# Second layer's first FFN: 19 pairs of up chunks as 2x2 block products with seven multiplications, its modulation computed in other FFNs

## The chip, the core and the metric

The program runs on one core of one Trainium2 chip. The metric is the device time of one execution in microseconds (us). Engines: TensorE (PE, with its weight loads PEld), VectorE (DVE), ScalarE (ACT), GpSimd (POOL) and SyncE (SP), which issues the DMAs here.

## The reference, cut to what matters

Two transformer blocks are computed on 256 tokens ("latent") with 256 context tokens beside them in the first block, model width 1024. The first block has two layers; each layer has a feed-forward network (FFN), a token mixer and a second FFN. Everything is float32.

```python
def _swiglu(h, w1, w3, w2):                       # w1, w3: 1024 x 2816, w2: 2816 x 1024
    return (jax.nn.silu(h @ w1) * (h @ w3)) @ w2
def _modulation(cond, w, b):                      # nine vectors of 1024 per layer
    m = jax.nn.silu(cond) @ w + b
    return [m[:, None, j * D_MODEL:(j + 1) * D_MODEL] for j in range(N_MOD)]
...
    for l in range(DEPTH):                        # DEPTH = 2
        ml = _modulation(c, w_ada[l], b_ada[l]); mc = _modulation(c_ctx[None], w_ada[l], b_ada[l])
        ffn1 = (ffn1_w1[l], ffn1_w3[l], ffn1_w2[l])
        lat = lat + 0.5 * ml[2] * _swiglu(_modulate(lat, norm_ffn1_g[l], ml[0], ml[1]), *ffn1)
        cx = cx + 0.5 * mc[2] * _swiglu(_modulate(cx, norm_ffn1_g[l], mc[0], mc[1]), *ffn1)
        ...                                       # token mixer, then ffn2 in the same way
```

## The kernel before

Activations lie transposed, features on partitions and tokens along the free axis: columns 0 to 255 are the latent tokens, 256 to 511 the context. A float32 product is made of three TensorE passes over operands split into a rounded part (hi) and a remainder (lo): hi times hi, hi times lo, lo times hi (`mm3`, lines 294 to 296).

**Weights** come in 544 chunks of up to 128 x 1024 in the order of `plan()`. For each, SP loads a raw tile (four buffers), ACT writes hi (line 145, six buffers) and DVE writes lo = raw - hi (line 156, five buffers). `take` hands the next chunk to the matmuls; `ahead_hi` and `ahead_lo` convert ahead as far as the buffers go.

**An FFN** has 22 pairs of up chunks: pair j holds 128 columns of w1 and the same of w3. They go in thirds of 8, 7 and 7 pairs (`THIRDS`), and each third is followed by eight w2 chunks that take the third's results. An up chunk is 8 k-blocks x 3 passes = 24 matmuls of 512 columns. `gated` (lines 519 to 527) then makes g = silu(first) * second: silu on ACT, the product on DVE (line 523), hi on ACT (line 525), lo on DVE (line 526). The results of w2 chunks are added to xT by DVE (line 417). In a layer's first FFN the first two pairs are computed together with the norm ahead of it (`norm_group`, `tail`).

**The order** is written out by hand: the schedule is manual, and each engine takes its instructions in the order in which the code issues them. `step` issues a chunk's matmuls, then the epilogue of the step before (`flush`), then conversions of hi (`ahead_hi`), one item of background work (`tick`), then conversions of lo (`ahead_lo`). There are six PSUM buffers `mm` of 512 columns, five temporaries `t`, and nine buffers `g`.

**Modulation.** The nine vectors of each layer come from 72 units of 128 outputs. A unit is one DMA of 512 KB and two DVE instructions over 1024 columns (line 279) with a read of the accumulator behind each. `ada` is a generator that does one unit per tick. The first layer's first FFN does the first layer's units 16 to 71, its second FFN does the second layer's units 0 to 39, and the second layer's first FFN does units 40 to 71.

Of the kernel before, what the change touches and what calls it, by code (L numbers as in the profile page):

```python
# [7 lines left out]
F32 = mybir.dt.float32  # L8
# [93 lines left out]


EARLY = 5
PACE = ([0, 1.25], [0, 1])


class Pair:


    def __init__(self, hi, lo=None):
        self.t = [hi, lo]
# [5 lines left out]
class Weights:  # L118


    def __init__(self, nc, flat, rawp, hlp, sizes, nraw, nhl):
        self.nc, self.flat, self.rawp, self.hlp = nc, flat, rawp, hlp
        self.sizes, self.nraw, self.nhl = sizes, nraw, nhl
        self.offs = np.concatenate([[0], np.cumsum(np.array(sizes) * 128)]).tolist()
        self.n = len(sizes)
        self.n_dma = self.n_hi = self.n_lo = self.n_take = 0
        self.raw, self.hl = {}, {}

    def dma_to(self, i):
        while self.n_dma <= min(i, self.n - 1):  # L130
# [6 lines left out]
            self.n_dma += 1  # L137

    def hi_to(self, i):
        while self.n_hi <= min(i, self.n - 1):  # L140
            j = self.n_hi
            self.dma_to(j)
            c = self.sizes[j]
            t = self.hlp.tile([128, 1024], F32R, tag="hi", name="hi", bufs=self.nhl)
            self.nc.scalar.activation(out=t[:, :c], in_=self.raw[j][:, :c], func=AF.Copy)  # L145
            self.hl[j] = Pair(t)
            self.n_hi += 1

    def lo_to(self, i):
        while self.n_lo <= min(i, self.n - 1):  # L150
            j = self.n_lo
            self.hi_to(j)
            c = self.sizes[j]
            t = self.hlp.tile([128, 1024], F32R, tag="lo", name="lo", bufs=self.nhl - 1)
            w = self.hl[j]
            self.nc.vector.tensor_tensor(  # L156
                out=t[:, :c], in0=self.raw.pop(j)[:, :c], in1=w[:, 0, :c].bitcast(F32), op=ALU.subtract)
            w.t[1] = t
            self.n_lo += 1
        self.dma_to(self.n_lo - 1 + self.nraw)  # L160

    def take(self, n):
        self.base = self.n_take
        self.lo_to(self.n_take + n - 1)
        r = [self.hl.pop(self.n_take + i) for i in range(n)]
        self.n_take += n
        return r

# [2 lines left out]
        self.ahead_lo(rate)  # L171

    def ahead_hi(self, rate=3):
        self.hi_to(min(self.n_hi + rate - 1, self.base + self.nhl - 1))

    def ahead_lo(self, rate=3):
        self.lo_to(min(self.n_lo + rate - 1, self.base + self.nhl - 2))


def build(tc, T):  # L180
    nc = tc.nc
    vo, nvec = vec_plan()
    sizes = [p[3] * p[5] for p in plan()]
    PS = bass.MemoryType.PSUM
    with ExitStack() as ctx, tc.manual_schedule():
        pool = lambda name, bufs, **k: ctx.enter_context(tc.tile_pool(name=name, bufs=bufs, **k))
# [7 lines left out]
        b1 = ctx.enter_context(ExitStack())  # L194
        hp = b1.enter_context(tc.tile_pool(name="hp", bufs=1))

        W = Weights(nc, T["wflat"], rawp, hlp, sizes, 4, 6)
# [33 lines left out]
        def drain(g):  # L231
            if g in side:
                for _ in g:
                    pass
                side.remove(g)
# [18 lines left out]
                    nc.vector.tensor_scalar(sl, sl, 0.5, None, ALU.mult)  # L254
            modn[l] = n1

        def ada(l, t0, t1, adap, lead):

            todo, tiles = list(range(t0, t1)), []

            def load():
                if todo:
                    t = adap.tile([128, 1024], F32, tag="ada", name="ada")
                    nc.sync.dma_start(out=t, in_=T["adaT"][l, todo.pop(0)])
# [8 lines left out]
            for j in range(t0, t1):  # L273
                if j > t0:
# [32 lines left out]
        def flush():  # L307
            while epis:
                epis.pop(0)()
# [202 lines left out]
            return ps  # L512


        def ffn(l, i, halves, ps4, gp, end, xepi=None):
            t1 = halves[-1][1]
            g = {}

            def gated(j, pa, pb):
# [11 lines left out]
            for ti, (j0, nj) in enumerate(THIRDS):  # L531
                for j in range(j0, j0 + nj):
                    if j < 2:
                        continue
# [7 lines left out]
                flush()  # L542
                X = [g.pop(j) for j in range(j0, j0 + nj)]
                lastt = ti == 2
                if lastt:
                    prime(AF.Sqrt)
                if lastt and xepi:
                    new_h2()
                for o in range(6 if lastt and end else 8):
                    (w,) = W.take(1)  # L550
                    p = mm_ps()
# [8 lines left out]
                    step(lambda: mmA(p, w, X, nj, 0, t1), epi, 0 if lastt and xepi and o == 7 else 3)  # L560
                if lastt and end:
                    return end(nj, X)

# [421 lines left out]
        with ExitStack() as ph:  # L985
# [118 lines left out]
        def ffn_phase(l, i, halves, ps4, units, end):  # L1104
            with ExitStack() as ph:
                gp = ph.enter_context(tc.tile_pool(name="gp", bufs=9))
                if units:
                    adap = ph.enter_context(tc.tile_pool(name="adap", bufs=3))

                    bg = ada(*units, adap, 2)  # L1110
                    side.append(bg)
                r = ffn(l, i, halves, ps4, gp, end)
                if units:
                    drain(bg)
            return r

        def mix_phase(l, ps4):
# [778 lines left out]
```

## Time and profile before

| | us |
|---|---|
| median of three runs (2420.06 to 2422.99) | 2420.52 |
| the profiled execution | 2421.72 |
| its span, first to last instruction | 2419.9 |

| engine | busy, us | share of the span | instructions |
|---|---|---|---|
| PE | 2392.5 | 99% | 15240 |
| DVE | 1565.7 | 65% | 2498 |
| ACT | 1013.0 | 42% | 1649 |
| POOL | 58.5 | 2% | 102 |

The profile is one execution. A busy share is an average over the whole span; the start of one instruction minus the start of the one before it on its engine tells what it costs where they stand in a row. Matmuls are pipelined: each shows as longer than the distance to the next, so their rate is read from starts.

### The profile page before, as it was taken

Reading aid. Unit: us, or ns where it says so; the run is one execution under the profiler, and the core shown is the slowest. Engines: PE = TensorE matmul, PEld = TensorE weight load, DVE = VectorE, ACT = ScalarE, POOL = GpSimd, SP = SyncE. Lnnn points to the kernel's source line nnn. Section 1 sums busy time; section 2 is a strip of 40 time slices with the busy share of each in tenths; the row PEclk is TensorE's granted clock in tenths of the full one; section 3 lists DMA queues with packets and bytes.
Section 4 is the critical chain, followed back from the end, with each engine's and each line's share of the span. In section 5 each row is a group of like instructions: output and inputs, shape, how many; then the busy total and the mean of one; then the engine's idle time right before and its main releaser. Section 6 shows DMA issues by size and latency. Waiting matters only on the chain.

```text
span 2419.9 us, 37688 instructions
## 1 busy us (share of the span) xinstructions
PE 2392.5 (99%) x15240; PEld 2145.0 (89%) x15240; DVE 1565.7 (65%) x2498; ACT 1013.0 (42%) x1649; POOL 58.5 (2%) x102
## 2 busy tenths in 40 slices
PE   7999999999999999999999999999999999999999
PEld 5888888999888888898888899999999999999999
DVE  6777876736478784468763366765576676557753
ACT  4322223455342222342222353654467556446642
POOL 0000000000000000000000000000002000010000
PEclk9999999999999999999999999999999999999999
DMA  8555552312245453235543232345655365553653
GB/s 311 201 191 175 200 190 70 104 54 70 79 160 198 178 196 112 89 133 198 184 149 102 87 100 84 114 157 187 186 193 169 127 201 185 192 166 114 209 190 125
DMA packets 107791, 370.88 MB, mean 153 GB/s; under 512 B 11864, under 2 KB 18008, under 8 KB 107232
## 3 DMA queue, kind: packets, MB, share of 16 engines
q1 hardware_dynamic: 107616, 368.47, 44.9%
q8 instruction: 120, 1.97, 0.3%
q14 instruction: 55, 0.45, 0.1%
HBM read 367.36 MB, written 1.06 MB: 152 GB/s over the span
## 4 chain that ended last, share of the span: by engine, by line
PE 91%; DVE 3%; issue 3%; ACT 2%; DMA 0%; POOL 0%; POOLq 0%; SPq 0%; DVEq 0%; ACTq 0%
PE mm L295 26%; PE mm L296 26%; PE mm L294 26%; PE mm L655 2%; PE mm L1188 2%; PE mm L1189 2%; PE mm L1187 2%; DVE lo L156 1%; PE mm L850 1%; PE mm L849 1%; PE mm L851 1%; ACT hi L145 0%; PE aux L383 0%; PE mm L1284 0%; PE aux L369 0%
## 5 line engine op out<-in xcount | busy, mean ns | idle before, releaser
L294 PE MATMUL mm<-h,hi 128*128 128x512 f32 (+1 forms) x2460 | 834.6, 339 | 3.0 <-ACT h L410 1.9
L296 PE MATMUL mm<-h,lo 128*128 128x512 f32 (+1 forms) x2460 | 829.8, 337 | 0.4 <-DVE lo L156 0.2
L145 ACT ACTIVATE hi<-raw 128x1024 fp32r<-128x1024 f32 (+1 forms) x544 | 563.5, 1042 | 527.1 <-PE mm L295 312.5
L156 DVE TENSOR_TENSOR lo<-raw,hi 128x1024 fp32r<-128x1024 f32 (+1 forms) x544 | 652.3, 1205 | 141.1 <-issue 55.8
L295 PE MATMUL mm<-l,hi 128*128 128x512 f32 (+1 forms) x2076 | 722.6, 348 | 1.1 <-DVE l L1074 0.2
L294 PEld LDWEIGHTS mm<-h,hi 128*128 128x128 f32 x2460 | 465.0, 189 | 56.7 <-ACT h L410 2.2
L296 PEld LDWEIGHTS mm<-h,lo 128*128 128x128 f32 x2460 | 464.7, 189 | 55.0 <-DVE lo L156 1.2
L295 PEld LDWEIGHTS mm<-l,hi 128*128 128x128 f32 x2076 | 392.5, 189 | 56.1 <-DVE l L411 2.7
L294 PE MATMUL mm<-g,hi 128*128 128x256 f32 (+1 forms) x1258 | 409.3, 325 | 0.0
L295 PE MATMUL mm<-g,hi 128*128 128x256 f32 (+1 forms) x1258 | 408.8, 325 | 0.0
L296 PE MATMUL mm<-g,lo 128*128 128x256 f32 (+1 forms) x1258 | 408.8, 325 | 0.0
L279 DVE CUSTOM_DVE_ANT_0 jk<-ada,condb,vec 128x1024 f32<-128x1024 f32 x256 | 328.1, 1282 | 11.7 <-ACT condb L272 7.2
L295 PEld LDWEIGHTS mm<-g,hi 128*128 128x128 f32 x1258 | 236.8, 188 | 22.2
L294 PEld LDWEIGHTS mm<-g,hi 128*128 128x128 f32 x1258 | 236.9, 188 | 22.1
L296 PEld LDWEIGHTS mm<-g,lo 128*128 128x128 f32 x1258 | 236.8, 188 | 22.0
L525 ACT ACTIVATE g<-t 128x512 fp32r<-128x512 f32 (+1 forms) x88 | 50.9, 578 | 350.8 <-DVE t L523 350.8
L417 DVE SCALAR_TENSOR_TENSOR xT<-mm,mods,xT 128x256 f32<-128x256 f32 x192 | 86.0, 479 | 135.7 <-PE mm L296 135.5
L523 DVE TENSOR_TENSOR t<-t,mm 128x512 f32<-128x512 f32 (+1 forms) x88 | 54.6, 620 | 181.2 <-PE mm L296 179.1
L295 PE MATMUL mm<-h,hi 128*128 128x256 f32 x512 | 143.9, 281 | 0.0
L1187 PE MATMUL mm<-hi,h 128*128 128x256 f32 x384 | 111.2, 289 | 0.0
L1188 PE MATMUL mm<-lo,h 128*128 128x256 f32 x384 | 107.6, 280 | 0.1
L1189 PE MATMUL mm<-hi,h 128*128 128x256 f32 x384 | 107.4, 280 | 0.0
(295 smaller groups left out, 2406.7 us busy)
## 6 DMA issues: line engine op xcount, KB each, us to landing
raw<-wflat SPq DMA_DIRECT2D x480, 512.0 KB, 3.4
ada<-adaT SPq DMA_DIRECT2D x128, 512.0 KB, 4.3
raw<-wflat SPq DMA_DIRECT2D x64, 448.0 KB, 3.3
ada<-ada SPq DMA_DIRECT2D x16, 512.0 KB, 10.0
condb<-condb SPq DMA_DIRECT2D x3, 1024.0 KB, 9.5
xT<-xT SPq DMA_DIRECT2D x2, 1024.0 KB, 5.7
bias<-d SPq DMA_DIRECT2D x2, 1024.0 KB, 7.5
out<-t SPq DMA_DIRECT2D x8, 128.0 KB, 1.9
```

The lines of the kernel that those rows point to most:

```text
L145: self.nc.scalar.activation(out=t[:, :c], in_=self.raw[j][:, :c], func=AF.Copy)
L156: self.nc.vector.tensor_tensor(out=t[:, :c], in0=self.raw.pop(j)[:, :c], in1=w[:, 0, :c].bitcast(F32), op=ALU.subtract)
L279: nc.vector.tensor_tensor_reduce(out=jk, in0=t, in1=condb[:, c, :], scale=1.0, scalar=V(f"bada{l}")[:, j:j + 1], op0=ALU.mult, op1=ALU.add ...
L294: nc.tensor.matmul(out, whi, xhi, start=start, stop=False)
L295: nc.tensor.matmul(out, whi, xlo, start=False, stop=False)
L296: nc.tensor.matmul(out, wlo, xhi, start=False, stop=stop)
L417: nc.vector.scalar_tensor_tensor(out=xT[:, o, t0:t1], in0=ps[:, t0:t1], scalar=gate(l, i, o, 0 if t0 == 0 else 1), in1=xT[:, o, t0:t1], op ...
L523: nc.vector.tensor_tensor(out=m[:, :t1], in0=s[:, :t1], in1=pb[:, :t1], op=ALU.mult)
L525: nc.scalar.activation(out=t[:, 0, :t1], in_=m[:, :t1], func=AF.Copy)
L1187: nc.tensor.matmul(p[:, :256], xhi, whi, start=(k == 0), stop=False)
L1188: nc.tensor.matmul(p[:, :256], xhi, wlo, start=False, stop=False)
L1189: nc.tensor.matmul(p[:, :256], xlo, whi, start=False, stop=(k == 7))
```

## The change

The 19 pairs j = 3 to 21 of the second layer's first FFN are computed in another way. w1 and w3 of a pair are taken as two block rows, the two halves of the 1024 inputs as two block columns, and the latent and the context tokens as the two columns of the right side: a 2x2 times 2x2 block product, done with seven block multiplications in the form that needs four sums of weights and four of tokens. A block multiplication has 4 k-blocks x 3 passes = 12 matmuls of 256 columns.

Per pair, `Weights` makes four units instead of two: s1 is the first raw chunk as it is, s2, s4 and s3 come from sums that DVE makes in place in the raw tiles; each then gets hi and lo. s1 and s2 use the old buffers, s3 has two buffers and s4 one. `hold` keeps units that are used twice. `tokens` makes the token sums at the start of the FFN, `last_sums` writes the fourth over the context half of h after pair 2. `pair_of_seven` issues the products: z = s1 * b11, d = s2 * t0, then the seventh product of the pair before, then z += s4 * t2, d += s3 * b22, a = s1 * b21, z += s3 * t3; its own seventh product (z += s2 * t1) is issued after the first two of the next pair. ACT and DVE combine z, d and a between the products. After a third's last pair the first two w2 chunks are split so that its seventh product stands between their parts.

The modulation units leave this FFN: its units and those of the FFN before are done in the first layer's second FFN (units 8 to 71) and first FFN (0 to 7 of the second layer behind its own 56), eight units per seven ticks.

```diff
+FAST = {("ffn1", 1)}
+FIRST_FAST = 3
...
+            if p[0].endswith("_w1") and (p[0][:4], p[1]) in FAST and p[4] // 128 >= FIRST_FAST:
+                self.units += [("s1", j), ("s2", j), ("s4", j), ("s3", j)]
+                j += 2
...
+    def fits(self, u, part):
+        if u >= self.n:
+            return False
+        k, j = self.units[u]
+        if j + (k == "s2") > self.done - 1 + self.nraw:
+            return False
+        if k in ("s3", "s4"):
+            live = sum(self.units[v][0] == k for v in list(self.hl) + list(self.held) if v < u)
+            return self.sp is not None and live < self.room[k]
+        return self.ring[u] <= self.ring[self.base] + self.nhl - 1 - (part == "lo")
...
     def hi_to(self, i):
+        add = lambda o, a, b: self.nc.vector.tensor_tensor(out=o, in0=a, in1=b, op=ALU.add)
...
+            if k == "s2":
+                self.lo_to(u - 1)
+                a, b = self.raw[j], self.raw[j + 1]
+                add(a[:, 0:512], a[:, 0:512], b[:, 0:512])
+                add(b[:, 0:512], b[:, 0:512], b[:, 512:1024])
+            elif k == "s4":
+                self.lo_to(u - 1)
+                add(self.raw[j + 1][:, 512:1024], self.raw[j + 1][:, 512:1024], self.raw[j][:, 0:512])
+            elif k == "s3":
+                add(self.raw[j][:, 512:1024], self.raw[j][:, 512:1024], self.raw[j + 1][:, 512:1024])
+            s = self.source(u)
+            t = self.tile(u, "hi")
+            self.nc.scalar.activation(out=t[:, :s.shape[-1]], in_=s, func=AF.Copy)
...
     def ahead_hi(self, rate=3):
-        self.hi_to(min(self.n_hi + rate - 1, self.base + self.nhl - 1))
+        for _ in range(rate):
+            if not self.fits(self.n_hi, "hi"):
+                break
+            self.hi_to(self.n_hi)
...
-                yield 0
+                if n % 8 != 3:
+                    yield 0
...
+        def tokens(gp, tb):
...
+            for i in range(4):
...
+                sub(s[:, 1], s[:, 1], s[:, 0])
+                sub(s[:, 0], s[:, 3], s[:, 0])
+                nsum(s[:, 3], s[:, 3], s[:, 1])
+                nsum(s[:, 2], s[:, 3], s[:, 2])
...
+                nc.scalar.activation(out=th, in_=r, func=AF.Copy)
+                sub(tl, r, th[:, :].bitcast(F32))
...
+            def last():
+                for i in range(4):
+                    nc.scalar.activation(out=h[i][:, 0, 256:512], in_=t3[i], func=AF.Copy)
+                    sub(h[i][:, 1, 256:512], t3[i], h[i][:, 0, 256:512].bitcast(F32))
...
+                def context():
+                    plus(v, CT, z)
+                    nc.vector.tensor_tensor(out=v[0][:, CT], in0=u[0][:, CT], in1=v[0][:, CT], op=ALU.mult)
+
+                def final():
+                    m = v[0]
+                    nc.vector.tensor_tensor(out=m[:, LA], in0=u[0][:, LA], in1=z[:, :256], op=ALU.mult)
+                    t = gp.tile([128, 2, 512], F32R, tag="g", name="g")
+                    nc.scalar.activation(out=t[:, 0, :], in_=m, func=AF.Copy, scale=-1.0)
+                    nc.vector.scalar_tensor_tensor(
+                        out=t[:, 1, :], in0=m, scalar=-1.0, in1=t[:, 0, :].bitcast(F32),
+                        op0=ALU.mult, op1=ALU.subtract)
+                    g[j] = t
+
+                step(lambda: seven(z, s1, 0, b11, True), first, 1)
+                (s2,) = W.take(1, True)
+                step(lambda: seven(d, s2, 0, tsum(0), True), second, 1)
+                if before:
+                    step(*before(), 1)
+                (s4,) = W.take(1)
+                step(lambda: seven(z, s4, 0, tsum(2), False), lambda: copy(u, CT, z), 1)
+                (s3,) = W.take(1, True)
+                step(lambda: seven(d, s3, 1, b22, False), lambda: plus(u, CT, d), 1)
+                a = mm_ps()
+                step(lambda: seven(a, s1, 1, b21, True), upper, 1)
+                W.held.discard(unit)
+                step(lambda: seven(z, s3, 0, tt3, False), context, 1)
...
-            bg = ada(0, 16, 72, adap, 2)
+            bg = ada([(0, j) for j in range(16, 72)] + [(1, j) for j in range(8)], adap, 2)
...
-        r = ffn_phase(0, 2, H2, r, (1, 0, 40), lambda nk, X: tail(0, 2, nk, X, H2, 1, 0, H2))
-        r = ffn_phase(1, 0, H2, r, (1, 40, 72), lambda nk, X: tail(1, 0, nk, X, H2, 1, 1, H2))
+        r = ffn_phase(0, 2, H2, r, [(1, j) for j in range(8, 72)], lambda nk, X: tail(0, 2, nk, X, H2, 1, 0, H2))
+        r = ffn_phase(1, 0, H2, r, (), lambda nk, X: tail(1, 0, nk, X, H2, 1, 1, H2))
```

## Rows read from the trace of the kernel before

**Rows 1.** The page: busy us (share of the span) and instructions of each engine.
```profile
PE 2392.5 (99%) x15240; PEld 2145.0 (89%) x15240; DVE 1565.7 (65%) x2498; ACT 1013.0 (42%) x1649; POOL 58.5 (2%) x102
```
**Rows 2.** Windows: stretch, us, busy of PE, PEld, DVE, ACT, POOL, granted clock, DMA, GB/s.
```profile
77.00:362.00 285.00, 285.00 (x1223) 229.50 (x1222) 226.70 (x332) 71.87 (x88) 0.00 (x0) 1.00 0.54 191
705.00:750.00 45.00, 45.00 (x195) 36.24 (x194) 34.80 (x49) 14.42 (x17) 0.00 (x0) 1.00 0.53 191
...
1077.80:1133.80 56.00, 56.00 (x241) 45.16 (x240) 43.24 (x60) 17.45 (x21) 0.00 (x0) 1.00 0.52 185
1178.60:1257.00 78.40, 78.40 (x337) 63.23 (x336) 59.59 (x85) 20.80 (x27) 0.00 (x0) 1.00 0.50 171
1296.20:1374.60 78.40, 78.40 (x337) 63.22 (x336) 25.14 (x28) 20.80 (x27) 0.00 (x0) 1.00 0.28 88
```
**Rows 3.** Timeline of PE: first matmul of pair 2, of pair 3, of w2.
```profile
1066.60 0.40 PE L294 MATMUL mm<-h,hi 128*128 128x512 f32 x1
...
1077.80 0.40 PE L294 MATMUL mm<-h,hi 128*128 128x512 f32 x1
...
1133.80 0.40 PE L294 MATMUL mm<-g,hi 128*128 128x512 f32 x1
```
**Rows 4.** Timeline of PE: 256-column matmuls in a row, the first and the fourth.
```profile
2100.22 0.28 PE L294 MATMUL mm<-g,hi 128*128 128x256 f32 x1
...
2100.57 0.28 PE L294 MATMUL mm<-g,hi 128*128 128x256 f32 x1
```
**Rows 5.** Groups by form, DVE: busy us, mean ns, idle before and what ended it.
```profile
L156 DVE TENSOR_TENSOR lo<-raw,hi 128x1024 fp32r<-128x1024 f32 x480 | 582.8, 1220 | 129.1 <-PE mm L296 55.2 <-issue 44.1 <-ACT hi L145 29.7
...
L411 DVE SCALAR_TENSOR_TENSOR l<-t,mods,h 128x256 fp32r<-128x256 f32 x72 | 34.3, 481 | 6.4 <-ACT h L410 6.4
...
L1352 DVE TENSOR_TENSOR xT<-xT,mm 128x256 f32<-128x256 f32 x40 | 16.3, 418 | 22.2 <-PE mm L296 22.2
L358 DVE TENSOR_TENSOR acc<-acc,t 128x512 f32<-128x512 f32 x20 | 13.6, 680 | 0.0
...
L1507 DVE SCALAR_TENSOR_TENSOR D<-dist,lg,D 128x512 f32<-128x512 f32 x4 | 3.0, 752 | 0.1
```
**Rows 6.** Groups by form, ACT.
```profile
L145 ACT ACTIVATE hi<-raw 128x1024 fp32r<-128x1024 f32 x480 | 502.9, 1055 | 444.1 <-PE mm L295 298.6 <-issue 105.2 <-DMA raw<-wflat 22.4
...
L525 ACT ACTIVATE g<-t 128x512 fp32r<-128x512 f32 x66 | 41.7, 632 | 307.9 <-DVE t L523 307.9
...
L918 ACT COPY vt<-mm 128x256 f32<-128x256 f32 x16 | 6.0, 376 | 7.5 <-PE mm L851 7.5
```
**Rows 7.** Timeline: gating of pair 2 on DVE, ACT, DVE.
```profile
1078.07 0.69 DVE L523 TENSOR_TENSOR t<-t,mm 128x512 f32<-128x512 f32 x1 [4.11 <-PE mm L296]
...
1078.79 0.63 ACT L525 ACTIVATE g<-t 128x512 fp32r<-128x512 f32 x1 [5.03 <-DVE t L523]
...
1079.45 0.69 DVE L526 TENSOR_TENSOR g<-t,g 128x512 fp32r<-128x512 f32 x1 [0.70 <-ACT g L525]
```
**Rows 8.** Timeline of DVE: gating, a modulation unit, a lo, the next unit.
```profile
1101.85 0.69 DVE L526 TENSOR_TENSOR g<-t,g 128x512 fp32r<-128x512 f32 x1 [0.70 <-ACT g L525]
1102.46 1.28 DVE L279 CUSTOM_DVE_ANT_0 jk<-ada,condb,vec 128x1024 f32<-128x1024 f32 x1
...
1105.00 1.22 DVE L156 TENSOR_TENSOR lo<-raw,hi 128x1024 fp32r<-128x1024 f32 x1
1106.13 1.28 DVE L279 CUSTOM_DVE_ANT_0 jk<-ada,condb,vec 128x1024 f32<-128x1024 f32 x1
```
**Rows 9.** Timeline at the FFN's start: the last two lo, ACT's table load.
```profile
1063.30 2.36 DVE L156 TENSOR_TENSOR lo<-raw,hi 128x1024 fp32r<-128x1024 f32 x2 [1.02 <-PE mm L296]
...
1064.21 1.28 ACT L521 ACT_TABLE_LOAD   x1
```
**Rows 10.** Windows: a stretch at the other clock level.
```profile
1594.90:1605.10 10.20, 7.58 (x33) 7.06 (x33) 8.94 (x20) 6.19 (x12) 0.00 (x0) 0.50 0.30 103
```
**Rows 11.** Timeline of PE in that stretch, with the idle time before.
```profile
1598.74 0.58 PE L294 MATMUL mm<-h,hi 128*128 128x256 f32 x1 [1.91 <-ACT h L410]
```

More of the change, by code (lines that the diff above doesn't have):

```diff
@@ L137, in dma_to, with source, tile @@
             self.n_dma += 1
+    def source(self, u):
+        k, j = self.units[u]
+        if k == "n":
+            return self.raw[j][:, :self.sizes[j]]
+        return {"s1": self.raw[j][:, :], "s3": self.raw[j][:, :], "s2": self.raw[j + 1][:, :],
+                "s4": self.raw[j + 1][:, 512:1024]}[k]
+    def tile(self, u, part):
+        k = self.units[u][0]
+        if k in ("s3", "s4"):
+            return self.sp.tile([128, 1024 if k == "s3" else 512], F32R, tag=k + part, name=part, bufs=self.room[k])
+        return self.hlp.tile([128, 1024], F32R, tag=part, name=part, bufs=self.nhl - (part == "lo"))
@@ L140, in hi_to @@
         while self.n_hi <= min(i, self.n - 1):
[L141 to L146, printed above, removed]
+            u = self.n_hi
+            k, j = self.units[u]
+            self.dma_to(j + (k == "s2"))
+            if k == "s2":
[8 more added lines that the diff above has]
+                add(self.raw[j][:, 512:1024], self.raw[j][:, 512:1024], self.raw[j + 1][:, 512:1024])
@@ L150, in lo_to, with take @@
         while self.n_lo <= min(i, self.n - 1):
[L151 to L157, printed above, removed]
-            w.t[1] = t
+            u = self.n_lo
+            self.hi_to(u)
+            if self.n_lo > u:
+                continue
+            s = self.source(u)
+            c = s.shape[-1]
+            t = self.tile(u, "lo")
+            w = self.hl[u]
+            self.nc.vector.tensor_tensor(out=t[:, :c], in0=s, in1=w[:, 0, :c].bitcast(F32), op=ALU.subtract)
+            w.t[1] = t
+            k, j = self.units[u]
+            if k == "n":
+                self.raw.pop(j)
+                self.done = j + 1
+            elif k == "s3":
+                self.raw.pop(j), self.raw.pop(j + 1)
+                self.done = j + 2
             self.n_lo += 1
-        self.dma_to(self.n_lo - 1 + self.nraw)
-    def take(self, n):
-        self.base = self.n_take
+        self.dma_to(self.done - 1 + self.nraw)
+    def take(self, n, hold=False):
+        self.cur = self.n_take
         self.lo_to(self.n_take + n - 1)
         r = [self.hl.pop(self.n_take + i) for i in range(n)]
+        if hold:
+            self.held |= set(range(self.n_take, self.n_take + n))
         self.n_take += n
@@ L173, in ahead_hi @@
     def ahead_hi(self, rate=3):
-        self.hi_to(min(self.n_hi + rate - 1, self.base + self.nhl - 1))
+        for _ in range(rate):
+            if not self.fits(self.n_hi, "hi"):
+                break
+            self.hi_to(self.n_hi)
     def ahead_lo(self, rate=3):
-        self.lo_to(min(self.n_lo + rate - 1, self.base + self.nhl - 2))
+        for _ in range(rate):
+            if not self.fits(self.n_lo, "lo"):
+                break
+            self.lo_to(self.n_lo)
 def build(tc, T):
@@ L182, in build @@
     vo, nvec = vec_plan()
-    sizes = [p[3] * p[5] for p in plan()]
     PS = bass.MemoryType.PSUM
@@ L255, in ada_done, with ada @@
             modn[l] = n1
-        def ada(l, t0, t1, adap, lead):
-            todo, tiles = list(range(t0, t1)), []
+        def ada(cols, adap, lead):
+            todo, tiles = list(cols), []
             def load():
@@ L272, in ada @@
             nc.scalar.activation(out=condb, in_=condb, func=AF.Silu)
-            for j in range(t0, t1):
-                if j > t0:
+            for n, (l, j) in enumerate(cols):
+                if n:
                     load()
@@ L516, in ffn, with seven, pair_of_seven, plus @@
+        def ffn(l, i, halves, ps4, gp, end, xepi=None, tb=None):
             t1 = halves[-1][1]
             g = {}
+            if tb:
+                tt, last_sums = tokens(gp, tb)
+            def seven(ps, w, q, x, start):
+                for k in range(4):
+                    c = slice((4 * q + k) * 128, (4 * q + k + 1) * 128)
+                    xh, xl = x(k)
+                    wh, wl = w[:, 0, c], w[:, 1, c]
+                    for m, (a, b) in enumerate(((wh, xh), (wh, xl), (wl, xh))):
+                        nc.tensor.matmul(ps[:, :256], a, b, start=start and k + m == 0, stop=k == 3 and m == 2,
+                                         skip_group_check=not start)
+            b11 = lambda k: (h[k][:, 0, 0:256], h[k][:, 1, 0:256])
+            b21 = lambda k: (h[4 + k][:, 0, 0:256], h[4 + k][:, 1, 0:256])
+            b22 = lambda k: (h[4 + k][:, 0, 256:512], h[4 + k][:, 1, 256:512])
+            tt3 = lambda k: (h[k][:, 0, 256:512], h[k][:, 1, 256:512])
+            tsum = lambda n: lambda k: tuple(t[:, n * 256:(n + 1) * 256] for t in tt[k])
+            def pair_of_seven(j, before):
+                z, d = mm_ps(), mm_ps()
+                u, v = [], []
+                LA, CT = slice(0, 256), slice(256, 512)
+                unit = W.n_take
+                (s1,) = W.take(1, True)
+                copy = lambda t, c, ps: nc.scalar.copy(t[0][:, c], ps[:, :256])
+                def plus(t, c, ps):
+                    nc.vector.tensor_tensor(out=t[0][:, c], in0=ps[:, :256], in1=t[0][:, c], op=ALU.add)
+                def first():
+                    u.append(tmp())
+                    copy(u, LA, z)
+                def second():
+                    v.append(tmp())
+                    copy(v, CT, d)
+                def upper():
+                    plus(u, LA, a)
+                    nc.scalar.activation(out=u[0], in_=u[0], func=AF.Silu)
+                def context():
[23 more added lines that the diff above has]
+                step(lambda: seven(z, s3, 0, tt3, False), context, 1)
+                W.held.discard(unit + 3)
+                def rest():
+                    def f():
+                        seven(z, s2, 1, tsum(1), False)
+                        W.held.discard(unit + 1)
+                    return f, final
+                return rest
@@ L542, in ffn @@
                 flush()
+                lastt = ti == 2
+                early = []
+                if before:
+                    ws = W.take(2, True)
+                    early = [(w, mm_ps()) for w in ws]
+                    X = [g[j] for j in range(j0, j0 + nj - 1)]
+                    some = lambda w, p: lambda: mmA(p, w, X, nj, 0, t1, 0, nj - 1)
+                    step(some(*early[0]), None, 1)
+                    step(*before(), 1)
+                    step(some(*early[1]), None, 1)
+                    flush()
                 X = [g.pop(j) for j in range(j0, j0 + nj)]
-                lastt = ti == 2
                 if lastt:
```

83 lines of the change are left out of this document (69 added, 14 removed).

## The prediction, on record before the run

> **What bounds the kernel now.** The page first: TensorE is busy 99% of the span [rows 1]. The windows over the changed feed-forward block (FFN) come next: each of its three up-chunk stretches has PE busy for its whole length (56.0 of 56.0, 78.4 of 78.4 twice), DVE for 32 to 77% [rows 2]. The product boundaries say the same: two up chunks run from 1066.60 to 1077.80, the next ten to 1133.80 [rows 3]; one chunk is 24 matmuls of 512 columns, 5.60 us, so 0.233 us each and 11.20 us per pair of chunks. Everything of DVE and ACT lies under PE there. The question is whether it still does.
>
> **PE's part.** A pair is now 7 products x 4 k x 3 passes = 84 matmuls of 256 columns instead of 48 of 512. Three 256-column matmuls take 0.35 us [rows 4], so a product is 1.40 us and a pair 9.80. Gain if PE stays the bound: 19 x 1.40 = 26.6 us.
>
> **What DVE and ACT get.** Cost is read from durations [rows 5, 6], and from the distance of two starts where one DVE instruction follows another, about 0.08 less: 0.61 for 512 columns, 1.13 for 1024 [rows 8]; so 0.34 for 256 (0.40 scalar_tensor_tensor). Per pair, DVE before: two lo (2.26) and two gating operations (1.22), 3.5 us. After: five 512-column operations (four weight adds, s4's lo), three 1024-column lo, five 256-column combinations and one 512-column scalar_tensor_tensor (0.67): 3.05 + 3.39 + 1.70 + 0.67 = 8.8 us. ACT: three 1024 and one 512 hi, silu and copy, three PSUM copies of 0.38: about 6.1. Both are under 9.80, so by busy time alone the change wins. What counts is the order, because the engines take instructions in the order in which the code issues them: DVE's second gating operation stands and waits for ACT's copy [rows 7].
>
> **The loop.** Let t = 0 be the end of a pair's seventh product, where the next pair P starts product 3. PE to DVE costs 0.27 (next product at 1077.80, DVE at 1078.07), a hop between DVE and ACT 0.03 [rows 3, 7]. Reading step() and hi_to/lo_to for a middle pair, DVE's order is:
> - previous pair's final: multiply 0.27 to 0.69; ACT copy to 1.35; DVE subtract, next start 2.05.
> - product 3's step, s4 of pair P+1: add, ends 2.74; ACT hi 2.77 to 3.40; its lo stands directly behind the add and waits, 3.43; next start 4.04.
> - product 4's step, s3 of P+1: add to 4.73, hi 4.76 to 5.82, lo at 5.85, next 6.98.
> - product 5's step: d's combination 0.34, lo of s1 of P+2 (hi long done) 1.13: 8.45.
> - product 6's step: a's combination 0.34; two adds end 10.09; hi of s2 of P+2 10.12 to 11.18; lo 11.21, next 12.34.
> - next step: z's combination 0.42, ends 12.76.
>
> Product 7 of P accumulates onto the z that this last instruction reads, so PE may not start it before 12.81. PE has reached it at 8.40 (six products) and waits 4.4 us. It ends at 14.21, and only then can P's final multiply start: the chain closes. **Period 14.2 us** per full pair against 11.2 before: DVE's 8.8 us of work, about 3.5 us in which it waits for ACT, 0.3 of PE to DVE, and product 7 itself with nothing of DVE's queued beside it (two steps there issue no conversion: s4 has one buffer, and it is full).
>
> Not every pair is full. In the second half of a third's last pair but one only w2 chunks, without adds, are left to convert: 13.6 (here a's combination ends 8.87, silu, hi, lo, z's combination 12.14). The last converts almost nothing and is PE's: five products, 7.0. A third's first pair finds s1 to s3 converted during w2, but the next s4 can't be written before product 3 (2.8 to 4.2) has read the one s4 buffer, so its hi starts at 4.4 instead of 2.77: 15.8 to the end of its product 7, counted from its product 1.
>
> **The start.** tokens() stands in DVE's queue ahead of gating chunks 0 and 1. DVE is free at 1065.6 [rows 9]. Per i: four 256-column and one 512-column add or subtraction (1.97), two negated sums (0.88), ACT's 768-column copy with hops (between rows 6's two sizes, 0.90), the subtraction (0.87): 4.62, four times 18.5, to 1084.1. Table load 1.28 [rows 9] and silu free the first PSUM buffer at 1085; product 1 of the first pair needs it, and PE ended chunk 2 at 1077.80. Both gatings end at 1089.1, s2's adds, hi and lo at 1092.7 (product 2). Then the s4, s3, s1, s2 conversions, all issued in chunk 2's steps, to 1100.9, gating chunk 2 to 1102.9, the last sums to 1104.2. ACT's copy of z stands behind these, so product 3 starts at 1104.5. The loop from there, its s4 hi held until product 3 has ended (1106.1), ends product 7 at 1117.5: 39.7 us after 1077.8, where PE alone would take 12.6.
>
> **Sum.** First third: 39.7 + 2 x 14.2 + 13.6 + 7.0 = 88.7, before 56.0: +32.7. Second and third: 15.8 + 4 x 14.2 + 13.6 + 7.0 = 93.2, before 78.4: +14.8 each. Together +62.3. The w2 stretches cost what they did: the split of their first two chunks issues the same matmuls, PE covers the conversions there with 5.6 us a step.
>
> **The moved modulation.** One unit is 2.54 us of DVE (1102.46 to 1105.00, rows 8). Its 32 units in the changed FFN lay under a full PE [rows 2]; taking them out frees no time on the path: 0. In layer 0's second FFN 64 units instead of 40, eight per seven steps: per two steps 2 gating operations with their hop 1.9, two lo 2.3, 16/7 x 2.54 = 5.8, so 10.0 of 11.2. The first FFN already ran one unit per step with PE at 285.0 of 285.0 [rows 2]. In w2 steps (4.9 us) it is about even, and the chunks converted ahead (up to five lo buffers) are the cover. I take 0; without the cover, at the three ends of up chunks, at most one double unit each: 5.1 x 3 = 15 us. The added loads are 512 KB per unit at a DMA share of 0.54 [rows 2]: 0.
>
> **The clock.** In a stretch where PE had gaps, one of them 1.91 us, the granted clock was 0.50 (1.2 instead of 2.4 GHz) for 10.2 us [rows 10, 11]; in the thirds to be changed it is 1.00 [rows 2]. PE gets a 4.4 us gap in each of 16 pairs, and longer ones at the start. A product 7 at half clock is 1.4 us longer and lies on the loop: between 0 and 16 x 1.4 = 22. I take 4, nearer to 0, since a slow product 3 shortens the gap that follows. The Trainium skill ("TensorE: Matmul & The Clock Gate", section "HAM oscillation — how this bites in real kernels") says that matmul groups with idle between them can start at the half clock each time; rows 10 and 11 show one such fall. By that rule the 22 would be taken whole; that is rival C.
>
> Forecast against the profiled execution (2421.72, span 2419.9 and 1.8 around it): 2421.7 + 62.3 + 4 = 2488; the median of the runs is 1.2 lower, so **2487 us**. Its own range is 2466 to 2508: 0.5 us either way on 16 pairs (8) and half of the 27 us that the start loses (13).
>
> **Rivals.**
> - A, faster: the lead of one converted pair absorbs DVE's order and PE stays the bound: 2420.5 - 26.6 = 2394. For it: DVE's 8.8 us under 9.80. Against: the lead covers weights; z's combination isn't a weight and stands behind them in the queue. It decides at a chain of 8.4 us up to z's combination; I count 12.8. Below a period of 11.2 and with a start under 8 us lost it would be faster.
> - B: ACT's hops are filled by other DVE work, so the period is 8.8 + 0.3 + 1.4 = 10.5: thirds 39.7 + 21.0 + 10 + 7 = 77.7 and twice 12.4 + 4 x 10.5 + 10 + 7 = 71.4: +21.7 - 14.0 = +8, 2429. Against: lo follows its own add and hi in issue order.
> - C: every gap drops the clock: 2483 + 22 = 2505. For it: the 4.4 us gaps; against: a busy second half in every pair.
>
> **Chances.** Forecast 0.70, A 0.08, B 0.10, C 0.12. About 0.2% (5 us) is what a measurement here tells from no change: faster 0.09, same 0.03, slower 0.88. The range 2430 to 2512 leaves out A and half of B, 13 in 100, and the far ends of the others.
>
> **What would show it.** In the trace after: z's combination (DVE, 256 columns from mm) as the releaser of PE's first matmul of product 7, PE idle there about 4 us, 13 to 16 times; DVE idle 1.1 us before the lo of s2 and s3 and 0.7 before s4's; pair period 14.2; PE idle some 27 us between 1078 and 1118; PE busy in total 26 us less. Wrong, if PE is solid in the thirds (A), if the period is near 10.5 with DVE full (B), or if granted clocks of 0.50 fill the thirds (C).

## The result and the profile after

The changed kernel takes **2500.78 us** (median of four runs, 2498.9 to 2502.7) beside 2420.47 of the kernel before: ratio **1.033, 95% interval 1.0312 to 1.0347**. It is 80 us slower, where 67 were forecast; the time lies in the range given. Its profiled execution has a span of 2500.9 us, 81.0 over that of before.

The page of the changed kernel: busy time of each engine [rows 1 show it before], PE and the granted clock over the span in 40 slices, and the chain of waits by engine.
```profile
PE 2404.2 (96%) x15924; PEld 2193.2 (88%) x15924; DVE 1689.2 (68%) x2724; ACT 1065.9 (43%) x1751; POOL 61.2 (2%) x102
...
PE   7999999999999999968989799999999999999999
PEclk9999999999999999978989899999999999999999
...
PE 82%; DVE 9%; ACT 4%; issue 3%; DMA 1%; POOL 0%; POOLq 0%; SPq 0%; DVEq 0%; ACTq 0%
```
Beside the first slice, which reads 7 before as well, PE has holes in the slices of the changed FFN alone, and its clock falls in the same slices. PE does less work (the new products are shorter), yet its busy time is up by 11.7 us: part of it ran at half clock.

The windows of the changed kernel over its three up-chunk stretches, from the end of the chunk ahead of the first product to the first w2 chunk, with 1.4 more at the end for the last product 7, which stands between parts of w2 chunks; columns as in rows 2.
```profile
1076.85:1172.60 95.75, 63.29 (x416) 61.17 (x416) 60.00 (x92) 39.71 (x61) 0.00 (x0) 0.79 0.22 72
1217.30:1316.50 99.20, 82.75 (x584) 81.21 (x584) 58.88 (x90) 38.48 (x61) 0.00 (x0) 0.86 0.24 76
1355.70:1455.90 100.20, 80.97 (x583) 79.50 (x582) 58.89 (x90) 38.59 (x61) 0.00 (x0) 0.88 0.23 75
```
Against 56.0 and twice 78.4 [rows 2] that is +39.7, +20.8 and +21.8, together +82.3; the FFN begins 0.95 earlier. So the whole loss lies in these three stretches. The clock column, 1.00 before, is 0.79 to 0.88: the clock stood at 0.50 for 41.0, 27.3 and 23.9 us of them. DVE is the busiest engine behind PE and has no more than 63% of any of them.

The waits of PE in the changed FFN, and three of DVE's from 1060 to 1460 us (engine, line waited for: us in total, times, longest). L641 is the product, L660 a combination on DVE, L657 a PSUM copy on ACT, L712 the silu of the old pairs, L208 hi, L222 lo; L680 is the final multiply, L682 and L683 are the hi and lo of its result.
```profile
PE mm L641 <- DVE t L660: 47.0, 16, 4.0
PE mm L641 <- ACT t L657: 9.0, 1, 9.0
PE mm L641 <- ACT t L712: 8.1, 1, 8.1
PE mm L641 <- ACT hi L208: 3.6, 1, 3.6
PE mm L641 <- DVE lo L222: 0.5, 1, 0.5
```
```profile
DVE lo L222 <- ACT hi L208: 60.7, 54, 3.4
DVE t L680 <- PE mm L641: 29.2, 13, 2.6
DVE g L683 <- ACT g L682: 12.5, 18, 0.7
```
Sixteen times PE stands ahead of product 7 until z's combination has been done: 47 us. The other four lines are the start, 21.2 us, each once. DVE in turn spends 60.7 us standing at a lo for the hi of the same chunk, and 29.2 at the final multiply until product 7 has ended. (DVE's waits for w2 products, 24.5 us, lie under a busy PE.)

One period of the loop: DVE's timeline (start, duration, operation, idle before and its releaser). L680 is the final multiply, L191 a weight sum, L660 a combination.
```profile
1265.59 0.42 DVE L680 TENSOR_TENSOR t<-t,mm 128x256 f32<-128x256 f32 x1 [2.56 <-PE mm L641]
1266.70 0.69 DVE L683 SCALAR_TENSOR_TENSOR g<-t,g 128x512 fp32r<-128x512 f32 x1 [0.69 <-ACT g L682]
1267.31 0.69 DVE L191 TENSOR_TENSOR raw<-raw 128x512 f32<-128x512 f32 x1
1268.78 0.69 DVE L222 TENSOR_TENSOR lo<-raw,hi 128x512 fp32r<-128x512 f32 x1 [0.78 <-ACT hi L208]
1269.38 0.69 DVE L191 TENSOR_TENSOR raw<-raw 128x512 f32<-128x512 f32 x1
1271.20 1.23 DVE L222 TENSOR_TENSOR lo<-raw,hi 128x1024 fp32r<-128x1024 f32 x1 [1.13 <-ACT hi L208]
1272.34 0.42 DVE L660 TENSOR_TENSOR t<-mm,t 128x256 f32<-128x256 f32 x1
1272.68 1.21 DVE L222 TENSOR_TENSOR lo<-raw,hi 128x1024 fp32r<-128x1024 f32 x1
1273.81 0.42 DVE L660 TENSOR_TENSOR t<-mm,t 128x256 f32<-128x256 f32 x1
1274.14 1.41 DVE L191 TENSOR_TENSOR raw<-raw 128x512 f32<-128x512 f32 x2
...
1276.67 1.23 DVE L222 TENSOR_TENSOR lo<-raw,hi 128x1024 fp32r<-128x1024 f32 x1 [1.12 <-ACT hi L208]
1277.82 0.42 DVE L660 TENSOR_TENSOR t<-mm,t 128x256 f32<-128x256 f32 x1
```
Product 7 of the pair before ended at 1265.32 (the final multiply less 0.27), which is the prediction's t = 0. Three times DVE stands for a hop: 0.78, 1.13, 1.12 us, and 0.69 more for the final copy. The last line is what releases PE, at 1278.29. PE's side of the same period: the first product 7, then the windows over it, by granted clock.
```profile
1262.62 0.58 PE L641 MATMUL mm<-th,hi 128*128 128x256 f32 x1 [3.29 <-DVE t L660]
```
```profile
1262.62:1268.70 6.08, 6.08 (x28) 6.08 (x29) 2.12 (x4) 1.22 (x3) 0.00 (x0) 0.50 0.00 0
1268.70:1277.67 8.97, 6.91 (x58) 6.71 (x56) 6.61 (x9) 4.54 (x8) 0.00 (x0) 0.99 0.36 119
```
After the gap of 3.29 us PE runs for 6.1 us at the lower level (1.2 GHz), and product 7, which closes the loop, takes 2.7 instead of 1.40. The ends of the gaps in this third lie 15.66, 15.05, 15.67, 15.05 and 14.49 apart.

### The profile page after: what moved, and what is told of

Its sections match the earlier page's. It is cut to its first block, busy times and chain, and to the rows that moved or that the text cites. A ratio compares the mean times of both kernels' runs of the same rounds, so it can differ in the third digit from the quotient of the medians.

```text
span 2500.9 us, 39420 instructions
## 1 busy us (share of the span) xinstructions
PE 2404.2 (96%) x15924; PEld 2193.2 (88%) x15924; DVE 1689.2 (68%) x2724; ACT 1065.9 (43%) x1751; POOL 61.2 (2%) x102
## 4 chain that ended last, share of the span: by engine, by line
PE 82%; DVE 9%; ACT 4%; issue 3%; DMA 1%; POOL 0%; POOLq 0%; SPq 0%; DVEq 0%; ACTq 0%
PE mm L375 22%; PE mm L376 22%; PE mm L374 22%; PE mm L641 4%; DVE lo L222 3%; ACT hi L208 2%; PE mm L869 2%; PE mm L1407 1%; PE mm L1408 1%; DVE raw L191 1%; PE mm L1406 1%; PE mm L1063 1%; PE mm L1064 1%; PE mm L1065 1%; DVE t L660 1%
## 5 line engine op out<-in xcount | busy, mean ns | idle before, releaser
L222 DVE TENSOR_TENSOR lo<-raw,hi 128x1024 fp32r<-128x1024 f32 (+2 forms) x582 | 688.7, 1189 | 189.9 <-ACT hi L208 91.4
L208 ACT ACTIVATE hi<-raw 128x1024 fp32r<-128x1024 f32 (+2 forms) x582 | 593.1, 1029 | 523.8 <-PE mm L375 252.7
L374 PE MATMUL mm<-h,hi 128*128 128x256 f32 (+1 forms) x2156 | 713.7, 331 | 3.6 <-ACT h L490 2.4
L376 PE MATMUL mm<-h,lo 128*128 128x256 f32 (+1 forms) x2156 | 708.8, 329 | 0.4 <-DVE lo L222 0.2
L375 PE MATMUL mm<-l,hi 128*128 128x512 f32 (+1 forms) x1772 | 601.6, 339 | 1.1 <-DVE l L1288 0.2
L374 PEld LDWEIGHTS mm<-h,hi 128*128 128x128 f32 x2156 | 407.2, 189 | 43.4 <-ACT h L490 2.6
L376 PEld LDWEIGHTS mm<-h,lo 128*128 128x128 f32 x2156 | 407.0, 189 | 41.3 <-DVE lo L222 1.2
L375 PEld LDWEIGHTS mm<-l,hi 128*128 128x128 f32 x1772 | 334.8, 189 | 42.5 <-DVE l L491 2.7
L641 PE MATMUL mm<-th,hi 128*128 128x256 f32 x228 | 79.8, 350 | 59.6 <-DVE t L660 47.0
L641 PEld LDWEIGHTS mm<-th,hi 128*128 128x128 f32 x228 | 56.6, 248 | 63.6 <-DVE t L660 50.2
L1406 PE MATMUL mm<-hi,h 128*128 128x256 f32 x384 | 111.1, 289 | 0.0
```

Of the source, the lines that this page charges most:

```text
L208: self.nc.scalar.activation(out=t[:, :s.shape[-1]], in_=s, func=AF.Copy)
L222: self.nc.vector.tensor_tensor(out=t[:, :c], in0=s, in1=w[:, 0, :c].bitcast(F32), op=ALU.subtract)
L374: nc.tensor.matmul(out, whi, xhi, start=start, stop=False)
L375: nc.tensor.matmul(out, whi, xlo, start=False, stop=False)
L376: nc.tensor.matmul(out, wlo, xhi, start=False, stop=stop)
L641: nc.tensor.matmul(ps[:, :256], a, b, start=start and k + m == 0, stop=k == 3 and m == 2, skip_group_check=not start)
```

## The experiments

Line numbers shift by a few from kernel to kernel; the names of tiles tell the operations. "Before" is the kernel before on the same chip.

**The modulation move alone.** The new FFN is switched off; the units stay where the change has put them.
```diff
-FAST = {("ffn1", 1)}
+FAST = set()
```


> Only the moved modulation: no pair is computed with seven products. If it is hidden under PE, as I hold, the time is that of before, 2420.5 within 3 us. If the denser ticks break through at the ends of the up chunks, up to 15 us more, 2424 to 2435; if taking the units out of the changed FFN had freed something, less than 2417.

Measured 2420.83 (2419.73 to 2421.91) beside 2421.2, ratio 1.000 (0.9991 to 1.0010). The window over layer 0's second FFN, where units now go two at a time:
```profile
705.00:1002.00 297.00, 297.00 (x1275) 239.13 (x1274) 254.65 (x376) 76.68 (x93) 0.00 (x0) 1.00 0.56 200
```
PE is busy for all of it, with DVE at 86%. The move costs nothing and gives nothing; all 80 us are the products'.

**The gap filled with matmuls.** 24 matmuls of 256 columns, whose result nobody reads, ahead of each product 7.
```diff
+WARM = 24
...
+x = aux_ps()
+for n in range(WARM):
+    nc.tensor.matmul(x[:, :256], s2[:, 0, 512:640], h[4][:, 0, 0:256],
+                     start=n == 0, stop=n == WARM - 1)
 seven(z, s2, 1, tsum(1), False)
```


> As the changed kernel, but PE does 24 more matmuls of 256 columns (2.8 us, their result unused) just ahead of each pair's seventh product, where it waits for z's combination. If the gaps drop the clock and that makes the period 15.3 on average instead of the 14.2 of the walk, the granted clock stays at 1.00 in the thirds and the time falls to about 2484, with more work done. If the clock takes no part, 2500; if PE were the bound, 19 x 2.8 = 53 us more, 2553.

Measured 2496.72 (2496.59 to 2498.11), ratio 1.0313 (1.0298 to 1.0329): 4 us less than the changed kernel with 2.8 us more of PE's work per pair. All four of its times lie under all four of the changed kernel, but the intervals of the two ratios overlap: the gain is small, and the clock is what this run shows. The windows of this kernel over one period and from 1109.1 on:
```profile
1262.00:1276.43 14.43, 13.09 (x110) 12.89 (x109) 9.31 (x15) 5.76 (x9) 0.00 (x0) 1.00 0.23 74
1109.10:1480.00 370.90, 356.40 (x2501) 331.28 (x2501) 213.71 (x324) 132.42 (x195) 0.00 (x0) 1.00 0.27 86
```
The clock stays at the upper level and a full pair's period is 14.43 each time. The expected 2484 was missed by 12.7: I had not counted that in the last pair of each third, where PE is the bound, the added 2.8 us are not hidden (product 7 comes 2.8 us later behind the first w2 matmul there than in the changed kernel): 3 x 2.8 = 8.4. Most of the rest is the period, 14.43 and not 14.2. Less the 8.4, the kernel at full clock would be at 2488.3, so the clock costs about 12.5 us in the loop. That is worked out, not run. The two profiled executions give 14.7: up to the first w2 matmul the thirds take 94.28, 97.74 and 98.85 us in the changed kernel, 90.61, 92.77 and 92.79 here.

**lo one step later.** In this FFN a lo is issued only in the step after its hi.
```diff
 def ahead_hi(self, rate=3):
+    self.old_hi = self.n_hi
...
+    if self.sp is not None and self.n_lo >= (self.old_hi or 0):
+        break
```


> As the changed kernel, but in this FFN the lo of a unit is issued one step after its hi, so that it doesn't stand directly behind the add and the hi it waits for. By the walk the chain up to z's combination falls from 12.8 to 9.1 us, the period from 14.2 (with the clock's falls 15.3) to 10.6, PE's gap to under 1 us, the clock stays up; the start stays. Sum: +20 in the first third, -6 in each other, about 2430. If DVE's busy time or the seventh product's own wait were the cause, the time stays near 2500.

Measured 2435.15 (2434.05 to 2436.25), ratio 1.0058 (1.0043 to 1.0073): 66 of the 80 us are gone, with the same instructions. PE's waits in the FFN:
```profile
PE mm L645 <- ACT t L661: 8.4, 1, 8.4
PE mm L645 <- ACT t L716: 8.1, 1, 8.1
PE mm L645 <- DVE t L664: 5.2, 10, 0.6
PE mm L645 <- ACT hi L209: 3.6, 1, 3.6
PE mm L645 <- DVE lo L223: 0.5, 1, 0.5
```
The wait for z's combination has gone from 47.0 to 5.2 us, and the start has stayed. The clock is 1.00 from 1110.7 on. This shows the loop's cause: lo standing behind its own sum and hi. With it the clock's share goes too: the gaps that are left in the loop are 0.4 to 0.6 us. The edit has a price behind the FFN: until 1453.8, where the token mixer begins, PE waits 2.1 us for a lo, which the changed kernel doesn't do; every version with the later lo below has this wait.

**Product 7 into a PSUM bank of its own.** PE then needn't wait for z; DVE adds the two.
```diff
 def context():
+    copy(v, LA, z)
     plus(v, CT, z)
...
-    nc.vector.tensor_tensor(out=m[:, LA], in0=u[0][:, LA], in1=z[:, :256], op=ALU.mult)
+    plus(v, LA, e[0])
+    nc.vector.tensor_tensor(out=m[:, LA], in0=u[0][:, LA], in1=m[:, LA], op=ALU.mult)
...
-        seven(z, s2, 1, tsum(1), False)
+        e.append(aux_ps())
+        seven(e[0], s2, 1, tsum(1), True)
```


> As the changed kernel, but the seventh product goes to a PSUM bank of its own and is added by DVE afterwards (one DVE addition and one ACT copy more per pair), so PE needn't wait for z's combination before it. By the walk DVE's queue with its hops is then the bound alone: 13.0 us a period, 16 x 1.2 = 19 us less and perhaps the clock's falls, 2463 to 2482. If the wait on z alone were the lock, the period would be PE's 9.8 and the time about 2421.

Measured 2473.41 (2473.15 to 2474.02), ratio 1.0216 (1.0201 to 1.0231). It removes 27 us, with a period of 13.5 us.
```profile
PE mm L641 <- ACT t L657: 43.0, 25, 9.0
```
PE now waits for ACT's copies (the start's 9.0 among them): DVE's and ACT's queues with their hops are too long for 9.80 even when product 7 is no part of the circle. The wait named in the profile was where the queue's length showed, not all of its cause.

**The start.** The token sums are spread as background over pairs 2 to 5, and the first fast pair is the seventh (16 fast pairs for 19).
```diff
-FIRST_FAST = 3
+FIRST_FAST = 6
...
+def spread():
+    for i in range(4):
+        rest = sums(i)
+        yield 0
+        rest()
+        if i < 3:
+            yield 0
...
+    side.append(sums)
...
+if j == FIRST_FAST:
+    epis.append(last_sums)
```
`sums(i)` issues a block's sums and ACT's copy, `rest` its subtraction; `side` gives one item a tick; the last sums come after the third product. This FFN has eight buffers `g` instead of nine here.

> As the changed kernel, but the token sums are spread over the four plain pairs 2 to 5 (background work behind the gating of chunks 0 and 1), seven products begin at pair 6, and the last sums are issued after the third product of that pair. Order of conversions as in the changed kernel. If the start loses what the walk says, the first third loses its 40 us (plain pairs 44.8, then some 17 and 7, against 67.2) and the rest stays: 2421 + 2 x 20 + 1 = 2462, up to 2470 if DVE falls behind in the plain pairs. If the start were harmless, the time would fall only by the clock's part and the fewer slow pairs, to about 2485.

Measured 2467.71 (2466.78 to 2468.53), ratio 1.0194 (1.0180 to 1.0208). The start's waits are gone but for 1.0 us; those for the combination are 40.7 in 13. The first w2 matmul of the first third comes at 1136.0, beside 1133.8 before [rows 3] and 1171.1 as changed.

**Both.** The two edits above, the later lo and the spread start, in one kernel.

> The start of the run before (token sums spread, pairs from 6 on) together with lo one step after its hi. If both losses are separate and the walk holds: thirds two and three 74 each against 78.4, the first about even: 2411, between 2408 and 2420, faster than before. If something else bounds, 2425 to 2435.

Measured **2413.53** (2412.13 to 2415.11) beside 2420.79, ratio **0.9971 (0.9960 to 0.9982)**: 7 us faster than the kernel before, and 87 faster than the changed one. (Alone the two edits gave 66 and 33, together 99; the loss of three slow pairs, an estimated 12, is in both.) Its waits of PE in the FFN, and the window over one period:
```profile
PE mm L656 <- DVE t L675: 4.6, 9, 0.6
PE mm L380 <- DVE lo L223: 2.2, 2, 2.1
PE mm L656 <- ACT t L672: 2.0, 1, 2.0
```
```profile
1210.68:1221.49 10.81, 10.26 (x84) 10.06 (x84) 9.40 (x14) 5.66 (x10) 0.00 (x0) 1.00 0.30 99
```
DVE is busy for 9.40 of 10.81 us and stands 0.70 for the final copy. Of the 1.40 us a pair that seven products save, 0.39 (11.20 - 10.81) are left in the loop. The second of the waits, 2.1 us, is that behind the FFN which came with the later lo.

Five attempts to get the rest followed, on top of this version (the third of them on top of the second).

**Both, and product 7's own bank.** The edits of three diffs above.

> The run before with the seventh product in a bank of its own as well. The wait of 0.55 us per pair for z's combination goes; DVE has 9.1 us of work and one hop of 0.7 left in a period, so PE's 9.8 to 10.0: thirds of 71 against 78.4, the first a little under 67.2: 2405, between 2399 and 2412. If DVE's extra addition and ACT's extra copy cost more than the wait, as long as the run before or longer.

Measured 2427.25 (2426.86 to 2428.89), ratio 1.0029 (1.0018 to 1.0040): a miss, 14 us slower than without it. PE's waits in the FFN, then DVE's in a stretch of 70 us:
```profile
PE mm L656 <- ACT t L672: 17.9, 20, 2.0
```
```profile
DVE t L675 <- ACT t L672: 7.7, 6, 1.4
```
The added copy stands behind s2's hi in ACT's queue; DVE's combination waits 1.4 us for it, and the period is 12.33. I had counted the wait it removes and not the place of the copy it adds.

**Another order of conversions.** None in the steps of products 1, 6 and 7.
```diff
-step(lambda: seven(z, s1, 0, b11, True), first, 1)
+step(lambda: seven(z, s1, 0, b11, True), first, 0)
...
-    step(*before(), 1)
+    step(*before(), 0)
...
-step(lambda: seven(z, s3, 0, tt3, False), context, 1)
+step(lambda: seven(z, s3, 0, tt3, False), context, 0)
```

> Spread start and lo one step later, and the sums, hi and lo of s2 moved from the sixth product's step behind z's combination (no conversions in the steps of the sixth, first and seventh product). By the walk z's combination comes at 8.0 us instead of 9.1, before PE asks for it at 8.4; DVE has 8.8 us of work and one hop of 0.7 in a period, so PE's 9.8 to 10.0 is the bound: about nine full periods of 10.8 fall by 0.9, 2413.5 - 8 = 2405, between 2400 and 2410. If DVE's order isn't what the 0.57 us waits come from, 2413.

Measured 2420.75 (2419.08 to 2423.17), ratio 1.000 (0.9992 to 1.0009): a miss too, period 11.74.
```profile
PE mm L656 <- ACT t L672: 12.8, 19, 2.0
```
With the hi packed into fewer steps, ACT's PSUM copies stand behind them.

**The same, with the first fast pair the fifth.**
```diff
-FIRST_FAST = 6
+FIRST_FAST = 4
```

> The same with seven products from pair 4 instead of pair 6: two pairs more at 1.4 us less each, but DVE has the token sums, two pairs' gating and the first conversions (some 42 us) under 22 us of PE instead of 45. If the plain pairs are what covers the start, PE waits and this is slower than the run beside it by 3 to 12 us (2408 to 2417); if the start needs no cover, 3 us faster, 2402.

Measured 2436.25 (2435.87 to 2438.05), ratio 1.0065 (1.0050 to 1.0080): 15.5 us slower than the order alone. Two pairs more could have given at most 2.8 us; the token sums, with less time to be spread over, cost PE gaps of 1.5, 0.6, 6.1, 0.4, 2.9 and 0.4 us at the start, and 17.1 us there at clock 0.50. The start needs its cover.

**A third order.** No conversions in the steps of products 1, 2 and 3; s4, s3, s1, s2 in those of 4 to 7.
```diff
-step(lambda: seven(z, s1, 0, b11, True), first, 1)
+step(lambda: seven(z, s1, 0, b11, True), first, 0)
...
-step(lambda: seven(d, s2, 0, tsum(0), True), second, 1)
+step(lambda: seven(d, s2, 0, tsum(0), True), second, 0)
...
-step(lambda: seven(z, s4, 0, tsum(2), False), lambda: copy(u, CT, z), 1)
+step(lambda: seven(z, s4, 0, tsum(2), False), lambda: copy(u, CT, z), 0)
```

> Spread start, lo one step later, and the conversions moved to the steps of the fourth (s4), fifth (s3), sixth (s1) and seventh product (s2), none in the steps of the first, second and third: each of ACT's copies out of PSUM then stands ahead of the conversions in ACT's queue, and z's combination comes at 8.2 us, before PE asks for it at 8.4. If the waits of the two orders tried before are queue order alone, PE's 9.8 to 9.9 is the period: about nine full periods of 10.8 fall by 0.9, 2413.5 - 8 = 2405, between 2401 and 2410. If DVE's work (8.8 us and one hop) can't be packed into 9.8 in any such order, 2411 to 2416.

Measured 2414.46 (2410.59 to 2415.85), ratio 0.9971 (0.9960 to 0.9981): no different from the plain version, period 10.94.

**The weight sums on GpSimd.**
```diff
-add = lambda o, a, b: self.nc.vector.tensor_tensor(out=o, in0=a, in1=b, op=ALU.add)
+add = lambda o, a, b: self.nc.gpsimd.tensor_tensor(out=o, in0=a, in1=b, op=ALU.add)
```


> Spread start and lo one step later (the faster version so far), with the four weight sums of a pair made by GpSimd instead of DVE. In that version DVE is busy 9.4 of a period of 10.8 us, the rest being its hops; if DVE's work is the bound that is left, 2.4 us less of it lets PE's 9.8 be the period, about nine periods of 0.9 less: 2413.5 - 8 = 2405, down to 2400. If a GpSimd sum over 512 columns takes longer than 2 us, or slows DVE beside it, hi waits for it instead: 2411 to 2425.

Measured 2429.2 (2428.57 to 2429.76), ratio 1.0035 (1.0021 to 1.0049). Groups by form from 1180 to 1250 us (busy us, mean ns, idle before), first of this kernel, then of the one with the sums on DVE:
```profile
L192 POOL TENSOR_TENSOR raw<-raw 128x512 f32<-128x512 f32 x22 | 30.3, 1377 | 40.4 <-DVE lo L223 39.5
...
L223 DVE TENSOR_TENSOR lo<-raw,hi 128x512 fp32r<-128x512 f32 x6 | 8.1, 1357 | 5.0 <-ACT hi L209 4.6
L675 DVE TENSOR_TENSOR t<-mm,t 128x256 f32<-128x256 f32 x16 | 6.7, 418 | 0.6 <-PE mm L656 0.6
L691 DVE TENSOR_TENSOR t<-t 128x256 f32<-128x256 f32 x5 | 6.1, 1211 | 0.5
```
```profile
L192 DVE TENSOR_TENSOR raw<-raw 128x512 f32<-128x512 f32 x21 | 14.5, 690 | 0.5
...
L223 DVE TENSOR_TENSOR lo<-raw,hi 128x512 fp32r<-128x512 f32 x6 | 4.2, 693 | 2.9 <-ACT hi L209 2.7
...
L691 DVE TENSOR_TENSOR t<-t 128x256 f32<-128x256 f32 x6 | 2.6, 425 | 0.6
```
A sum takes 1.38 us there for 0.69, and DVE operations with both inputs in SBUF get longer (1357 for 693 ns, 1211 for 425), while the combination, with one input in PSUM, keeps its 418. The Trainium skill ("SBUF — State Buffer", section "Who interferes with whom") says that a VectorE instruction with two SBUF inputs contends with a GpSimd instruction that reads SBUF; these rows agree. A period of this kernel, and DVE's longest wait in it:
```profile
1219.81:1231.85 12.04, 10.26 (x85) 10.06 (x85) 8.59 (x11) 5.76 (x10) 5.54 (x4) 1.00 0.27 89
```
```profile
1231.56 1.23 DVE L223 TENSOR_TENSOR lo<-raw,hi 128x1024 fp32r<-128x1024 f32 x1 [2.26 <-ACT hi L209]
```
Without four sums DVE is still busy for 8.59 us, where it was 9.40 with them, and it stands 2.26 for s2's hi, which itself waited for two sums of together 2.71 us on GpSimd; ACT's copy, which releases PE, comes behind that hi. So the sums on the chain have got longer, and so have DVE operations beside them; how the 16 us divide between the two isn't shown.

## Why the prediction was right, and where it was off

**The mechanism held, step by step.** Rows of the period above, from t = 0 at 1265.32, with the forecast behind: s4's lo 3.46 (3.43), the next sum 4.06 (4.04), s3's lo 5.88 (5.85), d's combination 7.02 (6.98), a's 8.49 (8.45), product 7 released at 12.97 (12.81). The releaser is z's combination, sixteen times. The later lo, which changes nothing but the place of lo in DVE's queue, takes back 66 us; that settles it against rival A (the lead absorbs the order) and against rival B (period 10.5 with DVE full), which is where that edit arrives: 10.8. The wait itself is 2.9 us on average (47.0 in 16) where 4.4 was forecast: matmuls at half clock fill part of it.

**The start held.** Forecast: 39.7 us from the end of the last plain chunk to the end of the first product 7, with PE idle some 27 in it. The trace has 42.2 us (1076.85 to 1119.06, the final multiply at 1119.33 less 0.27), with 23.6 idle: the four waits of 21.2, and 2.4 ahead of product 7 instead of the loop's full gap. The rest of the excess is products at half clock. Spreading the sums takes back 33 us, of which three fast pairs fewer are an estimated 12 (periods of about 15.2 for 11.2 us).

**The modulation held**: 0, by its own run.

**The clock was mis-sized.** I took 4 of 0 to 22, on the reason that a slow product 3 shortens the gap that follows. In the trace 15 of the 16 gaps have 3.4 to 6.8 us at 0.50 at or just behind their end, and product 7 comes first behind the gap. It costs about 12.5 us in the loop (14.7 by the profiled executions), between the 4 taken and the 22 of rival C. So rival C's mechanism is real and lies on top of the forecast's; at 2505 it came nearer to the time than my 2487. The step that failed is the reason for the 4: what the slow product 3 takes from the gap does not pay for the slow product 7 ahead of it. The Trainium skill ("TensorE: Matmul & The Clock Gate", section "HAM oscillation — how this bites in real kernels") has groups of matmuls with idle between them start at the half clock each time; this trace agrees, with 0.50 behind 15 of 16 gaps.

**A hop was mis-sized.** With the clock held up the period is 14.43 and not 14.21: behind s4's sum ACT's hi starts 0.11 us after the sum's end (1264.41 after 1263.62 + 0.68 in the run with the gap filled), where I had 0.03, and the two sums of s2 take 1.41, where I had 1.30. Sixteen times 0.2 is 3 us, an estimate, since not all of the 16 are full.

Together: clock 8.5 over what was taken, hops 3, start 2.5, about 14 us; the median is 13.8 above the forecast. All three lie on the same side, so none hid another; the clock's share is known to some 2 us only.

**One sign was wrong**: PE's busy time was to fall by 26 us and has risen by 11.7. At half clock a busy engine is a slow one. In the version with both edits, at full clock and with 16 pairs, it falls to 2373.8, by 18.7 where 16 x 1.40 is 22.4.

What stays open: whether an order exists that packs DVE's 9.2 to 9.4 us per pair into PE's 9.80. The best two stand at 10.8 and 10.9, both with the final multiply's hop of ACT in them (0.70 and 1.31). Not run either: the later lo in the seven-product pairs alone, which might save the 2.1 us behind the FFN.

## What to carry to other kernels

An engine that takes its instructions in order is not free because its busy share is below one: walk one period of its queue in issue order, with every hop to another engine as time in which it stands, and see when the instruction arrives that the busiest engine needs. A consumer issued directly behind its producer's producer makes such a hop bare; one step later most of it is hidden (DVE's waits for hi fell from 60.7 to 14.6 us here). Gaps on TensorE that come back in every round, like these of 2 to 4 us, may have to be charged twice, once as idle time and once as the slow matmuls behind them, above all where these close the loop.

## What was not expected of the hardware

- The granted clock fell to 0.50 at each of the loop's 15 gaps of 2.1 to 4.0 us, although PE was busy for 11 to 13 us between two of them, and came back each time within 7 us; at the one of 1.5 us it didn't fall. In the loop of the run with the gap filled (gaps of 1.33 us) and of the version with both edits (0.6) it stayed at 1.00. So 2.8 us of useless matmuls per pair made the kernel no slower, and by the medians 4 us faster. The length of a gap alone doesn't decide: with product 7 in its own bank five gaps of 2.0 to 2.2 us in the second third had no fall, and one of 1.7 in the third had.
- A GpSimd sum of 512 columns takes 1.36 us (mean of 64), and a VectorE multiply of 256 columns beside it 1.21 us instead of 0.43: taking four sums (4 x 0.61 us) per pair off DVE made the kernel 16 us slower.
